# A hybrid attention and retention step: later stores of turned rows, and a later split of one left operand

## The chip, the cores and the metric

The kernel runs on one core of a Trainium2 chip. The metric is the device time of one execution in microseconds; before the change its median over three runs is 2233.36 us. The engines go by the short names of the profile: PE (matmul), PEld (weight load), DVE (VectorE), ACT (ScalarE), POOL (GpSimd), SP (SyncE, which here only issues DMAs). ACT and POOL issue DMAs too, in the order of their own instruction streams.

## What is computed

One layer of a streaming encoder, for 1024 new frames of a prompt and for 16 new frames of each of 8 running streams. One input projection gives queries, keys, values and gates for two groups of eight heads. Group A is stick-breaking attention, group B is retention with decay. Each head's output is normalised, multiplied by a gain and a gate, and all go through one output projection.

```
h = rms_norm(x, norm_pre)
q_sb, k_sb, v_sb, gate_sb, q_r, k_r, v_r, gate_r = project(h, w_in, pos)
o_sb = stick_breaking_block(q_sb, k_sb, v_sb, ...)
o_r, s = retention(q_r, k_r, v_r, s0, log_gamma)
y = concat(head_rms_norm(o_sb, g_sb) * silu(gate_sb), head_rms_norm(o_r, g_r) * silu(gate_r))
x = x + rms_norm(einsum('bte,ed->btd', y, w_out), norm_post)
```

D_MODEL is 2048, heads are 128 wide, everything is float32 in and out. The new keys, values and retention states are outputs as well.

## The kernel before

**Precision.** Each float32 operand of a large product is split into a high part (ACT, L174) and a low part (DVE, L175), and three matmuls (high by high, high by low, low by high) replace one. So each weight tile costs a load, an ACT copy, a DVE subtract, and then matmuls of 512 columns.

**Stages.** Tokens are in two groups: group 0 has prompt tiles 0 to 3 and the tile of samples, group 1 has prompt tiles 4 to 7. For each group and each head five panels run: a row panel (`project_rows`, L473: values and gates) and four column panels (`project`, L416), most often in the order retention keys, retention queries, attention queries, attention keys. Then comes the output stage: the output projection is one level of a seven-product scheme over 2 by 2 blocks (`product`, matmuls at L1306, L1309 and L1310). Products are numbered 1 to 7 and each has two halves of columns, `nh`. Their left operands are rows or sums of rows of the heads' outputs, split by `left`; their right operands are blocks or sums of blocks of the output weights, split by `load_split` two blocks ahead of use (`AHEAD` = 2).

**The planner.** All that is not a large matmul is written as generators, wrapped in `Job`. After each matmul of a panel `tick` advances a clock by one turn (by 0.75 turn in a row panel; in the output stage after every three matmuls by one, two or three turns) and lets at most one job that is due take its next step. What a step yields is the number of turns until its next step. `drain(job)` ticks until a job is done, with no matmul in between. The step only emits instructions in program order; the framework then orders each engine's stream. `pin` forbids an instruction to stand ahead of the latest large matmul at the time of its turn; it is an ordering rule and not a wait.

**The work around the first edit.** `finish` (L768) runs once per head and branch. It normalises and gates the head's rows on DVE, stores them to a scratch (`turn_out`), loads them back with 32 by 32 blocks moved (`turn_in`), transposes them on DVE (L782), multiplies by the gain (L783) and stores the turned rows to `s_y` with a DMA issued on ACT (L786). Between these are waits in turns: for group 1, 7 before `turn_out` (`D_HELD`), 16 more before `turn_in`, 13 before the transpose, 7 before the store. The tile names are `so` for attention and `ro` for retention. `drain(sb_job)` at L1230 stands in the next head's attention step, between its queries' and its keys' panel (behind both in the first head and the last two of group 1); `drain(ret_job)` at L1203 stands behind the next head's retention keys. Rows of `s_y` are read by `sum_rows` (sums of rows, L307) and by `left` (L344) in the output stage.

**The work around the second edit.** In the output stage `both` (L1463) makes the `left` jobs for a product and a list of groups. `left` loads rows into a ring (three buffers `mr` for group 0, two `yr` for group 1), yields `wait`, and then splits eight pieces, one per step, into operands named `mh`/`ml` (group 0) or `ah`/`al` (group 1); after a second piece it loads the next pair into the freed buffer. The job for product 2, group 0, starts with the first half of product 1 for group 1 (two turns after every three matmuls, eight blocks of four turns), and `all_of(ready)` drains it before product 2.

Of the kernel before, what the change touches and what calls it, by code (L numbers as in the profile page):

```python
# [47 lines left out]
D_HELD = 7  # L48
# [16 lines left out]
D_LEFT = 24  # L65
D_SUM2 = (4, 6, 26)
D_SUM3 = (3, 3, 6)
MR = 3
# [26 lines left out]
def tile_hybrid_step(  # L95
# [48 lines left out]
    wp = ctx.enter_context(tc.tile_pool(name="wp", bufs=4))  # L144
# [27 lines left out]
    def split(hi, lo, src):  # L172
        return (
            nc.scalar.activation(hi, src, AF.Copy),  # L174
            nc.vector.tensor_tensor(lo, src, hi.bitcast(F32), ALU.subtract),  # L175
        )

    def split_pre(hi, lo, src, k):
        return (
            nc.scalar.activation(hi, src, AF.Copy, scale=pre[:, k : k + 1]),  # L180
            nc.vector.scalar_tensor_tensor(  # L181
                lo, src, pre[:, k : k + 1], hi.bitcast(F32), ALU.mult, ALU.subtract
            ),
        )

    def inv_rms(pool, ssq, n, name):
        shape = list(ssq.shape)
        v = pool.tile(shape, F32, name=f"{name}v")
        r = pool.tile(shape, F32, name=f"{name}r")
        u = pool.tile(shape, F32, name=f"{name}u")  # L190
        nc.vector.tensor_scalar(v, ssq, 1.0 / n, EPS, ALU.mult, ALU.add)
        nc.scalar.activation(r, v, AF.Sqrt)
        nc.vector.reciprocal(r, r)
        nc.vector.scalar_tensor_tensor(u, r, -0.5, r, ALU.mult, ALU.mult)
        nc.vector.tensor_tensor(u, u, v, ALU.mult)
        nc.vector.scalar_tensor_tensor(r, u, 1.5, r, ALU.add, ALU.mult)
        return r

    def pin(*made):
        if anchor[0] is not None:  # L200
            for ins in made:
                tc.add_manual_dep(
                    ins.ins,
                    anchor[0].ins.name,
                    mybir.DependencyInfo(mybir.DependencyClass.NoSync, mybir.DependencyReason.SCHED_ONLY),
                    reason="not ahead of the products",
                )
# [7 lines left out]
    def tied(ins):  # L215

        if phase[0] == 0 and anchor[0] is not None:
            tc.add_manual_dep(
                ins.ins,
                anchor[0].ins.name,  # L220
                mybir.DependencyInfo(mybir.DependencyClass.NoSync, mybir.DependencyReason.SCHED_ONLY),
                reason="tied to the products",
            )
# [80 lines left out]
    def sum_rows(gi, h):  # L304
        def load(r):
            for kk in range(2):
                pin(nc.sync.dma_start(r[:, 2 * kk : 2 * kk + 2].rearrange("p a n -> p (a n)"), y_of(gi, kk * H + h)[:, :512]))  # L307

        ops = ((3, 1, 3, "a"), (1, 0, 1, "s"), (0, 3, 0, "s"), (2, 2, 0, "s"))
        return load, ops, s_s[gi][h // 2][:, h % 2]  # L310
# [3 lines left out]
    def sums(pool, items, pace, bufs):  # L314

        def fetch(load):
            r = pool.tile([P, 4, 256], F32, name="br", tag="br", bufs=bufs)
            load(r)
            return r

        r = fetch(items[0][0])
        yield pace[2]
        for i, (_, ops, dst) in enumerate(items):
            nxt = fetch(items[i + 1][0]) if i + 1 < len(items) else None
            for o, a, b, how in ops:
                pin(nc.vector.tensor_tensor(r[:, o], r[:, a], r[:, b], ALU.add if how == "a" else ALU.subtract))
                yield pace[0]
            yield pace[1]
            pin(nc.scalar.dma_start(dst, r))
            stored[0] += 1  # L330
            r = nxt
            yield pace[2]

    def left(gi, n, hi, lo, bufs, tag, deep, wait, spare=None):
        src = LEFT[n]
        raw = []

        def load(pair, r=None):
            r = bufs.tile([P, 2, 256], F32, name=tag, tag=tag, bufs=deep) if r is None else r
            if src[0] == "y":  # L340
                rows = s_y[gi][src[1] * H // 2 + pair][:, :, src[2] * 256 : src[2] * 256 + 256]
            else:
                rows = s_s[gi][pair][:, :, src[1], :]
            pin(nc.sync.dma_start(r, rows))  # L344
            raw.extend((r[:, 0], r[:, 1]))

        for pair in range(deep):
            load(pair)
        yield wait
        ahead = deep  # L350
        if spare is not None:
            load(deep, spare.pop().rearrange("p t j d -> p (t j d)")[:, :512].rearrange("p (i n) -> p i n", i=2))
            ahead += 1
            yield 0
        for h in range(HT):
            pin(*split(hi[h], lo[h], raw.pop(0)))
            if h % 2 and h // 2 + deep >= ahead and h // 2 + deep < HT // 2:
                load(h // 2 + deep)
            yield D_OP
# [37 lines left out]
    def operand(pool, tags, n, **kw):  # L397
        made = [pool.tile([P, HT, n], F32R, name=t, tag=t, **kw) for t in tags]
        return [[t[:, h] for h in range(HT)] for t in made]
# [87 lines left out]
    with ExitStack() as s1:  # L487
# [46 lines left out]
        with tc.tile_pool(name="p0", bufs=2) as p0, tc.tile_pool(name="p0s", bufs=1) as p0s, tc.tile_pool(  # L534
# [97 lines left out]
            for piece, (o, m) in enumerate(X_PIECES[:2]):  # L632
                for w in range(KT // WQ):
# [3 lines left out]
                    for j in range(WQ):  # L637
                        k = w * WQ + j
                        hi, lo = (half[w][:, j, o : o + m] for half in mov)
                        made = split_pre(hi, lo, xc[:, j, :], k)  # L640
# [54 lines left out]
        def turn_out(src, tag, q=nc.scalar, held=False):  # L695

            s = scr.tile([src.shape[1], P, P], F32, name=tag)
            store = q.dma_start(s.rearrange("k q c -> q k c"), src)
            if held:
                pin(store)  # L700
            return s
# [3 lines left out]
        def turn_in(s, raw, q, last=None):  # L705

            for i in range(4):
                tied(
                    (last if last and i == 3 else q).dma_start(  # L709
                        raw[32 * i : 32 * i + 32, :].rearrange("p (k a) -> p k a", a=32),  # L710
                        s[:, :, 32 * i : 32 * i + 32].rearrange("k (j b) a -> b (k j) a", b=32),
                    )
                )
# [44 lines left out]
        class Out:  # L758
# [9 lines left out]
            def finish(self, b, gi, h, at, oT, dst):  # L768
                rs = inv_rms(op, self.ssq, P, "o")
                for i in range(self.nt):  # L770
                    nc.vector.scalar_tensor_tensor(
                        self.o[:, i, :], self.o[:, i, :], rs[:, i : i + 1], gated[gi, h][:, at + i, b, :], ALU.mult, ALU.mult
                    )
                if gi == 1:
                    yield D_HELD
                s = turn_out(self.o, f"s_o{b}_{h}_{self.nt}_{gi}", held=gi == 1)
                yield D_TO[phase[0]] - (D_HELD if gi == 1 else 0)
                flat = self.o.rearrange("p k d -> p (k d)")
                turn_in(s, flat, back[phase[0]])
                yield D_TI[phase[0]]  # L780
                n = self.nt * P
                tied(nc.vector.transpose(oT[:, :n], flat))  # L782
                nc.vector.tensor_scalar(flat, oT[:, :n], gains[:, b, h : h + 1], None, ALU.mult)  # L783
                if gi == 1:
                    yield D_HELD
                store = nc.scalar.dma_start(dst, flat)  # L786
                if gi == 1:
                    pin(store)
# [354 lines left out]
        summed, sampled, lefts, mine = [], [], [], {}  # L1143
        held_over, spare = [], []

        def kept(i):
            return [[half[i][:, h // 2, h % 2 * 256 : h % 2 * 256 + 256] for h in range(HT)] for half in mov]
# [18 lines left out]
        for gi, g in enumerate(GROUPS):  # L1166
            tiles, n, nt = g["tiles"], g["n"], len(g["tiles"])
# [161 lines left out]
        made = collections.deque()  # L1329
# [64 lines left out]
    with ExitStack() as s3:  # L1394
        c3 = s3.enter_context(tc.tile_pool(name="c3", bufs=1))
        rp = s3.enter_context(tc.tile_pool(name="rp", bufs=1))
# [26 lines left out]
        def complete(key, c):  # L1423
            o = area(key, c)
            square(key, c, o)
            yield D_FIN
            pin(nc.vector.tensor_tensor(o, o, gpost[:, c * 512 : (c + 1) * 512], ALU.mult))
            if len(ssqs[key][1]) == 4:
                finishing[key] = Job(finish(key), D_FIN)
# [33 lines left out]
        def both(n, groups):  # L1463
            made = []
            for g in groups:
                mine[g, n] = operand(c3, ("ah", "al"), 256, bufs=2) if g else kept(at[n])
                made.append(left(g, n, *mine[g, n], *((rp, "yr", 2) if g else (wp, "mr", MR)), D_LEFT // 2))
            return made

        def jobs_of(made):  # L1470
# [28 lines left out]
        def early_rows():  # L1499
            for key in LAST[:2]:  # L1500
                load_row(key)
                yield 30

        (first,) = both(1, G1)
        more = Job(sums(fp, [sum_rows(1, h) for h in range(EARLY, H)], D_SUM3, 3), 30)
        Job(load_gpost(), 40)
# [201 lines left out]
```

## Time and profile before

| | us |
|---|---|
| median of three runs | 2233.36 |
| lowest and highest of them | 2231.7 and 2233.37 |
| the profiled execution's own time | 2233.32 |
| its span, first to last instruction | 2231.6 |
| mean clock granted to PE, share of full speed | 0.998 |

The profile describes one execution. Its span leaves out what lies around the program. "Busy" of PE is made of matmuls whose ends are modelled, and matmuls overlap, so a busy PE says that it does not wait, not that it is at its peak. Rows of the waits name who waited for whom, then the total, the number of waits and the longest. Rows of a timeline give the start, the duration, the engine (with a q where it is the engine's sequencer that issues a DMA), the line, the tiles written and read, and in brackets how long the engine was idle before and what ended that. Rows of windows give the length of the window, the busy time and the number of instructions of each engine asked for, PE's granted clock, the DMA engines' busy share and GB/s.

### The profile page before, as it was taken

What the parts mean: (1) busy time and instruction counts of PE and PEld (TensorE: products, weight loads), DVE (VectorE), ACT (ScalarE), POOL (GpSimd) and SP (SyncE); (2) the same over time, 40 slices, a digit from 0 to 9 for tenths busy, and PEclk for the clock granted to TensorE, in tenths of its full rate; (3) what the DMA queues carried; (4) which work ended last, traced back from release to release, by engine and by line L of the source; (5) the groups of instructions that cost most, each with busy time, mean ns of one, the idle gap of its engine ahead of it and who ended that gap; (6) DMA issues with size and microseconds to landing.
All of it is one profiled execution on the core that took longest, in us unless ns stands there. A gap on an engine that the chain in (4) does not pass through costs nothing. (4 is left out here: it accounts for less than half of the span.)

```text
span 2231.6 us, 34775 instructions
## 1 busy us (share of the span) xinstructions
PE 2216.6 (99%) x12046; PEld 1887.5 (85%) x12046; DVE 1263.4 (57%) x2690; ACT 920.8 (41%) x1999; POOL 424.5 (19%) x715
## 2 busy tenths in 40 slices
PE   9999999999999999999999999999999999999998
PEld 8888889798888979888788888888888888878887
DVE  5435445453544545346566666757665757656677
ACT  6424333333333333334444343443434445545563
POOL 1022131222213122221222111120202212000020
PEclk9999999999999999999999999999999999999999
DMA  8567565576656557668768787878778777865785
GB/s 295 174 199 199 178 185 181 177 193 217 178 184 184 182 176 195 217 179 289 226 197 230 229 231 221 237 229 237 229 228 223 222 233 197 241 215 166 219 224 170
DMA packets 387234, 467.83 MB, mean 210 GB/s; under 512 B 126321, under 2 KB 243825, under 8 KB 386545
## 3 DMA queue, kind: packets, MB, share of 16 engines
q1 hardware_dynamic: 258928, 291.63, 44.2%
q0 software_dynamic: 36048, 94.67, 15.6%
q10 hardware_dynamic: 92080, 79.32, 11.3%
q8 instruction: 94, 1.54, 0.3%
q14 instruction: 84, 0.68, 0.1%
HBM read 364.56 MB, written 106.95 MB: 211 GB/s over the span
## 5 line engine op out<-in xcount | busy, mean ns | idle before, releaser
L473 PE MATMUL accm<-whn,ml 128*128 128x512 f32 x1152 | 452.3, 393 | 0.0
L473 PE MATMUL accm<-whn,mh 128*128 128x512 f32 x1152 | 451.6, 393 | 0.5 <-DVE rq L519 0.5
L473 PE MATMUL accm<-wln,mh 128*128 128x512 f32 x1152 | 451.9, 392 | 0.0
L174 ACT ACTIVATE wh<-wr 128x512 fp32r<-128x512 f32 x408 | 256.7, 631 | 466.2 <-PE acc L416 191.2
L416 PE MATMUL acc<-ml,wh 128*128 128x256 f32 (+2 forms) x1536 | 446.3, 341 | 0.7 <-DVE ml L181 0.3
L416 PE MATMUL acc<-mh,wl 128*128 128x256 f32 (+2 forms) x1536 | 443.9, 340 | 0.0
L416 PE MATMUL acc<-mh,wh 128*128 128x256 f32 (+2 forms) x1536 | 441.4, 338 | 0.2
L175 DVE TENSOR_TENSOR wl<-wr,wh 128x512 fp32r<-128x512 f32 x408 | 279.4, 688 | 264.6 <-ACT wh L174 244.7
L175 DVE TENSOR_TENSOR wln<-wrn,whn 128x512 fp32r<-128x512 f32 x256 | 175.5, 688 | 285.2 <-ACT whn L174 281.5
L174 ACT ACTIVATE whn<-wrn 128x512 fp32r<-128x512 f32 x256 | 161.2, 631 | 384.4 <-PE accm L473 261.4
L416 PEld LDWEIGHTS acc<-mh,wl 128*128 128x128 f32 x1536 | 281.3, 188 | 23.8 <-issue 5.4
L416 PEld LDWEIGHTS acc<-mh,wh 128*128 128x128 f32 x1536 | 283.0, 188 | 21.0 <-ACT mh L180 0.9
L416 PEld LDWEIGHTS acc<-ml,wh 128*128 128x128 f32 x1536 | 280.3, 188 | 21.1 <-DVE ml L181 1.6
L473 PEld LDWEIGHTS accm<-whn,mh 128*128 128x128 f32 x1152 | 216.5, 188 | 44.6 <-DVE rq L519 0.9
L473 PEld LDWEIGHTS accm<-whn,ml 128*128 128x128 f32 x1152 | 216.5, 188 | 43.2 <-issue 0.8
L473 PEld LDWEIGHTS accm<-wln,mh 128*128 128x128 f32 x1152 | 216.5, 188 | 43.2 <-DVE wln L175 0.3
L745 DVE TENSOR_TENSOR_SCAN kp<-kp 128x1152 f32<-128x1152 f32 (+4 forms) x40 | 82.6, 2064 | 55.9 <-POOL kp L734 28.1
L709 POOL DMA_DIRECT2D be<-s_be x120 | 87.8, 738 | 128.2 <-DMA s_be<-be 128.2
L1306 PE MATMUL a<-wh,mh 128*128 128x512 f32 x240 | 94.7, 395 | 0.1
L1309 PE MATMUL a<-wl,mh 128*128 128x512 f32 x240 | 93.8, 391 | 0.3 <-DVE wl L175 0.2
L1310 PE MATMUL a<-wh,ml 128*128 128x512 f32 x240 | 93.6, 390 | 0.0
L734 POOL TENSOR_SCALAR_AFFINE_SELECT kp<-kp 128x128 f32<-128x128 f32 x40 | 13.8, 345 | 369.2 <-ACT kp L728 369.2
(289 smaller groups left out, 3013.2 us busy)
## 6 DMA issues: line engine op xcount, KB each, us to landing
wrn<-w_rows SPq DMA_DIRECT2D x256, 256.0 KB, 3.9
wr<-w_cols SPq DMA_DIRECT2D x255, 256.0 KB, 4.4
kcT<-cache_k POOLq DMA_DIRECT2D x64, 512.0 KB, 4.7
vc<-cache_v SPq DMA_DIRECT2D x64, 512.0 KB, 5.3
wr<-s_b SPq DMA_DIRECT2D x80, 256.0 KB, 3.4
wr<-w_out SPq DMA_DIRECT2D x80, 256.0 KB, 4.3
br<-w_out SPq DMA_DIRECT2D x64, 256.0 KB, 4.6
s_b<-br ACTq DMA_DIRECT2D x32, 512.0 KB, 4.5
```

The lines of the kernel that those rows point to most:

```text
L174: nc.scalar.activation(hi, src, AF.Copy),
L175: nc.vector.tensor_tensor(lo, src, hi.bitcast(F32), ALU.subtract),
L416: last = nc.tensor.matmul(a[:, :m], lhs[:, j, :], rhs[w][:, j, o : o + m], start=(w == 0 and j == 0 and n == 0), stop=(w == KT // WQ - 1 a ...
L473: anchor[0] = nc.tensor.matmul(banks[t], lhs[q][:, j, ts], rhs, start=(k == 0 and n == 0), stop=(k == KT - 1 and n == 2),)
L709: (last if last and i == 3 else q).dma_start(raw[32 * i : 32 * i + 32, :].rearrange("p (k a) -> p k a", a=32), s[:, :, 32 * i : 32 * i + 3 ...
L734: nc.gpsimd.affine_select(blk, blk, pattern=[[-1, P]], base=0, channel_multiplier=1, compare_op=ALU.is_gt, fill=fill,)
L745: nc.vector.tensor_tensor_scan(rev, rev, rev, 1.0, ALU.mult, ALU.bypass)
L1306: ins = nc.tensor.matmul(a, hi[k][:, ts], wh, start=first, stop=False)
L1309: nc.tensor.matmul(a, hi[k][:, ts], wl, start=False, stop=False)
L1310: anchor[0] = nc.tensor.matmul(a, lo[k][:, ts], wh, start=False, stop=last)
```

## The change

Two constants change. The store of turned rows of group 1 is emitted 14 turns after its transpose and gain instead of 7. And the `left` job of product 2 for group 0 waits 16 turns instead of 12 between its first loads and its first split; all other `left` jobs keep their wait.

```diff
@@ -782,7 +782,7 @@
                 tied(nc.vector.transpose(oT[:, :n], flat))
                 nc.vector.tensor_scalar(flat, oT[:, :n], gains[:, b, h : h + 1], None, ALU.mult)
                 if gi == 1:
-                    yield D_HELD
+                    yield 2 * D_HELD
                 store = nc.scalar.dma_start(dst, flat)
                 if gi == 1:
                     pin(store)
@@ -1464,7 +1464,8 @@
             made = []
             for g in groups:
                 mine[g, n] = operand(c3, ("ah", "al"), 256, bufs=2) if g else kept(at[n])
-                made.append(left(g, n, *mine[g, n], *((rp, "yr", 2) if g else (wp, "mr", MR)), D_LEFT // 2))
+                more = 4 if (g, n) == (0, 2) else 0
+                made.append(left(g, n, *mine[g, n], *((rp, "yr", 2) if g else (wp, "mr", MR)), D_LEFT // 2 + more))
             return made
```

## The prediction

> **What bounds the kernel now.** I read the page first, then who waited for whom on PE, then busy time by stage, then the two places that the diff touches in order of time.
>
> ```profile
> span 2231.6 us, 34775 instructions
> PE 2216.6 (99%) x12046; PEld 1887.5 (85%) x12046; DVE 1263.4 (57%) x2690; ACT 920.8 (41%) x1999; POOL 424.5 (19%) x715
> ```
> ```profile
> PE pd L945 <- DVE kp L942: 1.5, 7, 0.5
> PE pb L565 <- DVE ones L538: 1.2, 1, 1.2
> PE a L1309 <- DVE wl L175: 1.0, 3, 0.7
> PE accm L473 <- DVE rq L519: 0.5, 1, 0.5
> PE pa L999 <- DVE so L851: 0.4, 1, 0.4
> PE acc L416 <- DVE ml L181: 0.3, 1, 0.3
> ```
> ```profile
> 1980.00:2020.00 40.00, 40.00 (x177) 32.76 (x176) 18.78 (x33) 15.04 (x33) 0.00 (x0) 1.00 0.44 139
> ```
> ```profile
> 2140.00:2180.00 40.00, 40.00 (x178) 33.12 (x177) 28.81 (x75) 27.94 (x64) 13.80 (x16) 1.00 1.00 236
> ```
>
> TensorE is the limit nearly everywhere. All its waits add to 1.5 + 1.2 + 1.0 + 0.5 + 0.4 + 0.3 = 4.9 us of 2231.6 (total, times, longest in each row). The first two rows lie outside both edits: the decode of group 0 and the start-up. Of what remains, the three waits for `wl` (1.0) and the one for `rq` (0.5) lie beside an edit. A change that moves instructions of other engines and removes no matmul can win a few of these waits and no more. It can lose more, if it makes PE wait where it does not wait now. In the two windows of the output stage that are shown PE is busy for 40.00 of 40.00 us, so what is won or lost before 1980 arrives at the end whole.
>
> **Edit 1, the store.** It moves sixteen issues (eight heads, two branches) by 7 turns. A turn is one tick of the planner: one matmul of a column panel, or 4/3 of one in a row panel. No instruction and no transfer is added. So the question is what sets the place of the store today, its turn or its data.
>
> ```profile
> L786 ACTq DMA_DIRECT2D s_y<-ro x16: 326/333/358, 203.8 to 1903.0; - x16
> L786 ACTq DMA_DIRECT2D s_y<-so x16: 326/338/363, 240.7 to 1928.5; - x16
> ```
> ```profile
> L344 SPq DMA_DIRECT2D yr<-s_y x12: 517/538/610, 1941.9 to 2147.2; - x12
> ```
> ```profile
> 1248.10:1296.85 48.75, 44.92 (x192) 35.78 (x192) 1.00 0.76 222
> ```
> ```profile
> 1296.90:1309.90 13.00, 11.54 (x48) 8.71 (x48) 1.00 0.80 225
> 1309.95:1322.40 12.45, 11.38 (x49) 9.05 (x49) 1.00 0.92 253
> 1322.40:1338.30 15.90, 12.88 (x49) 8.38 (x49) 1.00 0.80 236
> ```
> ```profile
> 1343.15 0.70 DVE L782 STREAM_TRANSPOSE be<-so 128x512 f32<-128x512 f32 x1
> ```
> ```profile
> 1344.15 0.48 DVE L783 TENSOR_SCALAR so<-be,pre 128x512 f32<-128x512 f32 x1
> ```
> ```profile
> 1344.54 0.63 ACT L174 ACTIVATE whn<-wrn 128x512 fp32r<-128x512 f32 x1 [2.10 <-PE acc L416]
> 1344.70 0.33 ACTq L786 DMA_DIRECT2D s_y<-so  x1
> ```
>
> I count the attention job of one head of group 1 that is made at about 1248. The next row panel has 192 matmuls at 0.75 turn, so 144 turns, at 44.92 / 192 = 0.234 us a matmul. Three column panels of 48 follow (a row with x49 counts an edge matmul twice), so the drain at L1230 comes at turn 288, near 1338.3. By the constants the job needs 11 + 11 turns to its first scores, 3 x 39 + 42 for four tiles, 2 x 21 for the two late steps, and 7 + 16 + 13 + 7 in `finish`: 22 + 117 + 42 + 42 + 43 = 266. I add about 5 turns for rounding to 0.75 and for turns that other jobs take: the store's turn is about 271, the 31st matmul of the third column panel, some 5 us before 1338. With 14 turns it is 278, some 3 us before it. But the trace has the store at 1344.70, 0.07 us after the gains that it stores ended (1344.15 + 0.48 = 1344.63), and behind an ACT split that belongs to the next row panel, whose turn is later than either. So data sets its place, about 9 us after the new turn. The same holds in the retention branch of the next head:
>
> ```profile
> 1350.01 0.39 PE L473 MATMUL accm<-whn,mh 128*128 128x512 f32 x1
> ```
> ```profile
> 1356.97 0.48 DVE L783 TENSOR_SCALAR ro<-rkn,pre 128x512 f32<-128x512 f32 x1
> ```
> ```profile
> 1358.25 0.34 ACTq L786 DMA_DIRECT2D s_y<-ro  x1
> ```
>
> That job is made at turn 192 and needs 11 + 23 + 28 to its first scores, 9 x 5 in the retention and 43 in `finish`: 342, 6 turns into the next row panel, which starts at turn 336 and at 1350.01. Held 14 it is 13 turns in, at 4/3 x 0.234 us a turn 4.1 us: 1354.1, again before its gains end at 1357.45. If the hold did bind in some heads, the store would leave 1.6 to 2.2 us later (7 turns). What hides that is distance: the last stores leave at 1903.0 and 1928.5, and `left` loads such rows of group 1 only from 1941.9 on. I cost edit 1 at 0.
>
> Its bounds. Below nothing: there is one place where an ACT that is held up by a store reaches PE, the wait for `rq`.
>
> ```profile
> 1753.61 0.34 ACTq L786 DMA_DIRECT2D s_y<-so  x1
> 1754.05 0.63 ACT L174 ACTIVATE whn<-wrn 128x512 fp32r<-128x512 f32 x1 [2.60 <-PE acc L416]
> 1754.70 0.60 ACT L517 ACTIVATE sw<-acc 64x512 f32<-64x512 f32 x1
> ```
>
> The split and the rope copy stand behind a store there. If the store went behind them, the copy could start up to 1 us sooner and the 0.5 us of PE would go: -0.5. Above nothing: the mechanism of rival B.
>
> **Edit 2, the split of group 0 for product 2.** The job starts with the first half of product 1 for group 1, 8 blocks of 4 turns. Its first loads stay at turn 1; the first split moves from turn 13 to 17, the eighth from about 27 to 31. Eight ACT copies and eight DVE subtracts move one block later, and with them SP's fourth load, which follows the second split.
>
> ```profile
> 1966.70 0.42 ACT L174 ACTIVATE mh<-mr 128x256 fp32r<-128x256 f32 x1 [2.76 <-DMA mr<-s_y]
> 1967.03 0.61 ACT L174 ACTIVATE wh<-wr 128x512 fp32r<-128x512 f32 x1
> ```
> ```profile
> 1970.05 0.63 ACT L174 ACTIVATE wh<-wr 128x512 fp32r<-128x512 f32 x1 [2.10 <-DMA wr<-w_out]
> ```
> ```profile
> 1967.15 0.43 DVE L175 TENSOR_TENSOR ml<-mr,mh 128x256 fp32r<-128x256 f32 x1 [0.95 <-ACT mh L174]
> 1967.50 0.68 DVE L175 TENSOR_TENSOR wl<-wr,wh 128x512 fp32r<-128x512 f32 x1
> ```
> ```profile
> 1967.19 0.39 PE L1306 MATMUL a<-wh,ah 128*128 128x512 f32 x1
> 1968.24 0.50 PE L1309 MATMUL a<-wl,ah 128*128 128x512 f32 x1 [0.66 <-DVE wl L175]
> ```
> ```profile
> 1970.90 0.40 PE L1306 MATMUL a<-wh,ah 128*128 128x512 f32 x1
> 1971.46 0.50 PE L1309 MATMUL a<-wl,ah 128*128 128x512 f32 x1 [0.16 <-DVE wl L175]
> ```
>
> The first split waits for its rows: ACT sits idle 2.76 us for the load, DVE 0.95 us for ACT, and the `wl` of block 6 is queued behind that `ml`. At 0.23 us between matmuls PE was due at 1967.42 and starts at 1968.24: 0.82 us late. Block 6's weights are split at turn 16 (two blocks ahead of use). So with the first split at turn 17 they stand ahead of it, `wl` runs about 0.95 us sooner, and this stall goes: -0.82.
>
> What is late next is the first block of the second half. Its `wh` starts at 1970.05 when its load has landed; `wl` and the PE row at 1971.46 hang on that. This load was issued ahead of all that moves, and the DMA engines had little room (the last two columns are DMA share and GB/s):
>
> ```profile
> 1964.10 4.47 SPq L1323 DMA_DIRECT2D wr<-w_out  x4
> 1968.88 0.52 SPq L344 DMA_DIRECT2D mr<-s_y  x1
> ```
> ```profile
> 1960.00:1970.00 10.00, 9.35 (x40) 6.79 (x39) 8.84 (x23) 4.45 (x12) 0.00 (x0) 1.00 0.88 301
> ```
>
> PE arrives there 0.82 us sooner and waits 0.82 us longer: +0.82. After that the moved splits compete with the weights of the second half. I take 0 for that, since the weights' splits have waits for loads around them that can absorb 0.4 us. Its ends: nothing below, and above it the late fourth load may hold ACT at the seventh split in front of a weight split, for up to the length of one block, 6 x 0.23 = 1.4 us.
>
> The Trainium skill, "DMA: Bandwidth & Descriptors", section "Anatomy of one DMA — SWDGE (gpsimd) path", fits a transfer as 2.0 us plus its bytes over 436 GB/s; for 256 KB that is an estimate of 2.6 us. By that the load of 1964.10 would land at 1966.7, the second stall would not hang on it, and the sum would be -0.8. This trace does not agree: its consumer began at 1970.05, after a wait for it.
>
> **Sum.** 0 for edit 1, -0.8 + 0.8 for edit 2: 0 on the span of 2231.6, and so on the 2233.3 of the profiled execution (1.7 us lie around the span), which is the median of the three runs (2233.4; 2231.7 to 2233.4). Small wins are likelier than small losses by the chances below, so I shade it by 0.2 and say **2233.2**.
>
> **Rivals.**
>
> A, a few waits are won. The second stall does not take the gain back, because the queue of transfers ahead of that load clears sooner. For: both PE waits are for `wl`, and DMA share is 0.88, not 1. Against: nothing ahead of the load changes its place. With the 0.5 of `rq`: -0.8 to -1.3, about 2232.1. The skill's formula would give this too.
>
> B, slower. The hold pushes `finish` past the drain at L1230. From there each missing turn is run with no matmul under it, and the retention job, which is in its middle then, loses cover between its PE, DVE, PE steps. It decides once more than 288 - 278 = 10 turns are lost beyond the 5 that I counted. Price: up to 7 turns x 0.234 = 1.6 us in each of 7 heads, 11 us: 2244. Against: twice the lost turns that I count would still fit.
>
> C, slower by little. The late fourth load holds ACT in front of a weight split: +1.4, about 2234.7.
>
> D, edit 1 does nothing, because data and not the turn places the store. That is inside my forecast.
>
> **How the numbers follow.** Forecast (2232.5 to 2234) 0.66, A 0.17, C 0.12, B 0.05. The range reaches over A and C and adds part of the spread of the runs, 1.7 us: **2230.7 to 2235.2**. A measurement of this kernel can tell about 0.2%, 4.5 us, from no change. The waits within reach (1.0 + 0.5 + 0.4) are less than that, so faster by more gets 0.02, the far end of A; slower by more is B, 0.05; the same 0.93.
>
> **What would show it.** Sixteen stores of group 1 at L786, each still at or after the end of its L783; retention matmuls around a drain spaced as now (else B). The PE wait near 1968 gone and the one near 1971.5 grown by as much (else A, or C if a new one follows it). PE without a gap from 1985 on. I would be wrong if PE waits where no row has a wait now, or if the order on ACT and DVE changes far from the two edits.

## The result, and the profile after

The changed kernel takes **2237.22 us** (median of 19 executions, 2234.96 to 2238.93) beside 2233.1 us (19, 2231.53 to 2235.43) for the kernel before. The ratio is 1.0017, with a 95% interval of 1.0011 to 1.0023: slower by 4.1 us. That is less than the 0.2% that the prediction calls no change, but it lies 2.0 us above the top of the forecast range.

The profiled execution of the changed kernel took 2235.51 us, 2.2 more than the profiled one before (2233.32), and lies near the low end of its 19. So this trace can show about half of the loss at most. Its head, and then its waits of PE (total, times, longest):

```profile
span 2233.8 us, 34771 instructions
PE 2216.3 (99%) x12046; PEld 1887.6 (85%) x12046; DVE 1263.8 (57%) x2690; ACT 920.7 (41%) x1999; POOL 424.0 (19%) x715
```
```profile
PE pa L848 <- DVE kp L811: 2.0, 1, 2.0
...
PE a L1309 <- DVE wl L175: 1.0, 3, 0.6
PE acc L416 <- ACT mh L180: 0.7, 2, 0.4
PE a L1306 <- ACT wh L174: 0.5, 1, 0.5
...
PE rs L980 <- DVE rq L521: 0.2, 1, 0.2
```

Busy times are as before. The large new wait is one of 2.0 us in **one** place of the attention of group 1, at L848. The rows left out are as before. Of the smaller new rows two are no sign of the edits. The 0.7 us at L180 stand in the first 100 us, ahead of both edits, and every other run but the kernel before shows 0.4 to 1.5 us there. The 0.5 us at L1306 stand at 1931.81, some 31 us before the first loads of edit 2's job, and e1, e3 and e4 below, which leave edit 2 out, have 0.2 to 0.6 us there:

```profile
1931.81 0.50 PE L1306 MATMUL a<-wh,mh 128*128 128x512 f32 x1 [0.51 <-ACT wh L174]
```

The windows (length, PE busy and its matmuls, clock, DMA share, GB/s) put the wait of L848 between 1400 and 1430 us and clear the stretches around it:

```profile
1000.00:1400.00 400.00, 400.00 (x2082) 1.00 0.79 233
1400.00:1430.00 30.00, 30.00 (x156) 1.00 0.99 260
1430.00:1955.00 525.00, 523.65 (x2524) 1.00 0.79 225
```
```profile
1000.00:1400.00 400.00, 400.00 (x2081) 1.00 0.79 234
1400.00:1430.00 30.00, 27.96 (x145) 1.00 0.89 238
1430.00:1955.00 525.00, 523.64 (x2523) 1.00 0.78 225
1980.00:2020.00 40.00, 39.76 (x174) 1.00 0.43 141
```

The first fence is the kernel before, the second the changed one. In 30 us PE lost 2.04 us; before and behind that, in group 1, nothing. The last row (40.00 of 40.00 before) has a small wait of the output stage, 0.23 us at 1983.18.

**The place near 1425 us.** These are the timeline rows of the kernel before, and then of the changed one: the transpose of L811, and on PE the last projection matmul and the matmuls of L848 that need the transpose.

```profile
1425.12 1.25 DVE L811 STREAM_TRANSPOSE kp<-be 128x1024 f32<-128x1024 f32 x1 [2.31 <-DMA be<-s_be]
```
```profile
1426.24 0.39 PE L416 MATMUL acc<-mh,wh 128*128 128x512 f32 x1
1426.47 1.12 PE L848 MATMUL pa<-vo,kp 128*128 128x128 f32 x8
```
```profile
1426.30 1.25 DVE L811 STREAM_TRANSPOSE kp<-be 128x1024 f32<-128x1024 f32 x1 [3.65 <-DMA be<-s_be]
```
```profile
1425.17 0.39 PE L416 MATMUL acc<-mh,wl 128*128 128x512 f32 x1
1427.60 1.16 PE L848 MATMUL pa<-vo,kp 128*128 128x128 f32 x8 [2.04 <-DVE kp L811]
```

Before, the transpose ended at 1425.12 + 1.25 = 1426.37 and PE reached L848 at 1426.47: a margin of 0.10 us, of which the rows of waits show nothing. After, PE is there at 1425.17 + 0.23 = 1425.40, and the transpose ends at 1427.55. On PE the eight matmuls of L848 stand behind 102 projection matmuls of this head instead of 106, so four earlier (4 x 0.23 = 0.9 us). The transfer that the transpose waits for lands later, which makes the remaining 1.3 us of this pair of traces.

Two traces exaggerate the second part. Nine of the fourteen traces have the old order, with 106: there the transpose ends between 0.10 us before PE arrives and 0.55 us behind, and PE's wait is at most 0.45 us. Five have the order with 102 (the change, e1, e4, e5, e9): there it ends 1.35 to 2.15 us behind. Counted from the last matmul of the row panel, it ends after 28.2 us on average in the nine and 28.7 us in the five. So 0.9 us of the wait come from the order in every case, and on average 0.5 us from the later landing.

**The place near 1970 us.** SP's issues in the output stage, first of the kernel before (the prediction shows the two rows ahead of these: four weight loads from 1964.10, the fourth `mr` at 1968.88), then of the changed one; then what SP waited for at L344 between 1960 and 1986 us, changed kernel:

```profile
1969.50 4.38 SPq L1323 DMA_DIRECT2D wr<-w_out  x4
1973.93 1.18 SPq L344 DMA_DIRECT2D yr<-s_y  x2
```
```profile
1965.06 4.49 SPq L1323 DMA_DIRECT2D wr<-w_out  x5
1972.22 0.52 SPq L344 DMA_DIRECT2D mr<-s_y  x1
1972.85 1.32 SPq L1323 DMA_DIRECT2D wr<-w_out  x2
1974.21 1.18 SPq L344 DMA_DIRECT2D yr<-s_y  x2
1975.49 7.99 SPq L1323 DMA_DIRECT2D wr<-w_out  x6
```
```profile
SPq L344 <- DVE ml L175: 2.6, 1, 2.6
```
```profile
SPq L344 <- DVE ml L175: 0.2, 1, 0.2
```

The last fence is the kernel before (1960 to 1985 us). The fourth load refills the buffer of the first pair, so it waits for the second split, `ml`. It waited 0.2 us; now it waits 2.6 us, and SP issues nothing between 1969.55 and 1972.22. Five weight loads now go ahead of it instead of four, so the fifth comes no later than before. What comes later is the fourth load itself, and behind it the eighth weight load, which feeds the last block of the second half: it now follows the two `yr` loads, at 1975.49, and stood ahead of them before. In this trace the ACT split of that block starts as its load lands, and PE waits for its low part at 1983.18 (0.23 us):

```profile
1981.77 0.63 ACT L174 ACTIVATE wh<-wr 128x512 fp32r<-128x512 f32 x1 [1.02 <-DMA wr<-w_out]
```

That wait alone proves nothing: e1, e3 and e5, without edit 2, have one of 0.22 to 0.23 us between 1980 and 1983 too. What edit 2 costs is read from the experiments. The Trainium skill, "Perfetto Trace Analysis", section "Summary: the profiler window per engine type", lists the actual data movement of a DMA that SP issues as hidden from the profile. The trace agrees: the row of the fourth load is 0.52 us long, from 1972.22, and the split that waits for its rows starts at 1975.67. The 2.6 us of waiting are not in the row either.

### The profile page after: what moved, and what is told of

It is laid out like the page before. It is cut to its first block, busy times and chain, and to the rows that moved or that the text cites. A ratio compares the mean times of both kernels' runs of the same rounds, so it can differ in the third digit from the quotient of the medians.

```text
span 2233.8 us, 34771 instructions
## 1 busy us (share of the span) xinstructions
PE 2216.3 (99%) x12046; PEld 1887.6 (85%) x12046; DVE 1263.8 (57%) x2690; ACT 920.7 (41%) x1999; POOL 424.0 (19%) x715
## 4 chain that ended last, share of the span: by engine, by line
PE 93%; DMA 3%; DVE 2%; issue 1%; ACT 1%; DVEq 0%; POOL 0%; ACTq 0%; SPq 0%; POOLq 0%
PE accm L473 35%; PE acc L416 33%; PE a L1309 4%; PE a L1310 4%; PE a L1306 4%; PE pa L848 2%; PE z L821 2%; PE pd L953 1%; PE zc L892 1%; DMA wr<-w_out 1%; PE rs L980 1%; PE pa L999 1%; PE pS L1016 1%; PE pa L1006 1%; DMA mr<-s_s 1%
## 5 line engine op out<-in xcount | busy, mean ns | idle before, releaser
L1306 PE MATMUL a<-wh,mh 128*128 128x512 f32 x240 | 94.8, 395 | 0.5 <-ACT wh L174 0.5
```

Source lines behind the costliest of these rows:

```text
L1306: ins = nc.tensor.matmul(a, hi[k][:, ts], wh, start=first, stop=False)
```

## The experiments

Three theories. **T**: the planner lets one job per turn take a step, so moving the store's step gives its old turn to another job and takes a turn from one; the order of the other work changes, and that makes the wait of L848. **S**: the later stores cost something themselves. **C**: edit 2 loses time since the fourth load is late and holds the weight loads in SP's queue. The expectations of e1 and e2 also name **L**: all of the loss is edit 2's. The experiments ran in three groups of four, each group beside its own runs of the kernel before (medians 2233.6, 2234.2 and 2234.27; 32 or 33 executions); each experiment has 11. What is "over before" is a difference of these medians.

A list of the planner's turns, written while the program is built, shows where T begins: turn, the turn at which the step was due, the job, and the wait that it yields. It is the second head of group 1. The numbers behind the names are lines of the program with the list built in, ten higher than in kernel.py. First the kernel before, then one in which that head's attention store alone is held:

```
4086.0 at 4086.0 due 2 residuals:405 wait 76 P1
4087.0 at 4086.0 due 2 sb_branch:1147>finish:795 wait None P1
4088.0 at 4087.0 due 1 sums:338 wait 26 P1
```
```
4086.0 at 4086.0 due 1 residuals:405 wait 76 P1
4087.0 at 4087.0 due 1 sums:338 wait 26 P1
...
4093.0 at 4093.0 due 1 sb_branch:1147>finish:795 wait None P1
```

The store was due together with another job's step, went one turn later, and pushed the weight sums (`sums`, L314) from 4087 to 4088. Held, it frees that turn. From there on the sums run ahead of where they were: by one turn, then two, in the end up to seven (eight in the changed kernel), and in the third head the attention job's steps come one turn earlier too: the one that emits these matmuls of L848 takes turn 4365 instead of 4366. Why one turn in the list becomes four matmuls in the order on PE was not followed up.

**e1, edit 1 alone.**

```diff
                 if gi == 1:
-                    yield D_HELD
+                    yield 2 * D_HELD
```

> Edit 1 alone (hold of 14 turns, the left operand as before). Theory T (turns): the planner lets one job step per turn, so moving the store's step by 7 turns moves the steps that it collided with, by one turn and then more, and with them the order of the PE stream in group 1; the attention matmuls of a head's last tile (L848) then stand ahead of their transposed weights (L811) and PE waits. All of the loss is in this edit: 2 to 5 us slower than before, with waits of L848 for L811. Theory L (left): the loss comes from edit 2; then this one is within 1 us of before.

2236.95 us (2234.36 to 2238.05), 1.001 (1.0001 to 1.0019): +3.3. Its waits of PE have the same new row, with 1.4 us:

```profile
PE pa L848 <- DVE kp L811: 1.4, 1, 1.4
```

L falls: edit 1 alone loses. The interval allows 0.2 to 4.2 us.

**e2, edit 2 alone.**

```diff
-                made.append(left(..., D_LEFT // 2))
+                made.append(left(..., D_LEFT // 2 + 4 * ((g, n) == (0, 2))))
```

> Edit 2 alone. Theory T: within 1 us of before; the PE wait near 1968 gone and the next one longer by about as much. Theory L: 2 to 5 us slower.

2235.44 us (2234.17 to 2239.74), 1.001 (1.0002 to 1.0019): +1.8. Both expectations missed: T had no loss of edit 2, L nearly all of it. Both edits lose, and 3.3 + 1.8 us can make up the whole 4.1, given that each is uncertain by about 2 us. The rows of DVE, ACT and PE, and the wait of SP:

```profile
1970.66 0.43 DVE L175 TENSOR_TENSOR ml<-mr,mh 128x256 fp32r<-128x256 f32 x1 [1.97 <-ACT mh L174]
```
```profile
1969.69 0.63 ACT L174 ACTIVATE wh<-wr 128x512 fp32r<-128x512 f32 x1 [1.79 <-DMA wr<-w_out]
1970.23 0.40 ACT L174 ACTIVATE mh<-mr 128x256 fp32r<-128x256 f32 x1
...
1975.96 0.42 ACT L174 ACTIVATE mh<-mr 128x256 fp32r<-128x256 f32 x1 [2.06 <-DMA mr<-s_y]
...
1976.76 0.41 ACT L174 ACTIVATE mh<-mr 128x256 fp32r<-128x256 f32 x1
1977.07 1.66 ACT L174 ACTIVATE wh<-wr 128x512 fp32r<-128x512 f32 x3
```
```profile
1977.74 0.50 PE L1306 MATMUL a<-wh,ah 128*128 128x512 f32 x1 [0.50 <-ACT wh L174]
1978.46 0.50 PE L1309 MATMUL a<-wl,ah 128*128 128x512 f32 x1 [0.23 <-DVE wl L175]
```
```profile
SPq L344 <- DVE ml L175: 2.9, 1, 2.9
```

The chain can be read off. The second split of `mh` (1970.23) now stands behind a weight split that waits 1.79 us for its own load. Its `ml` ends at 1971.09, and SP issues the fourth load at 1971.12 (1968.88 before). The seventh split needs these rows: ACT sits idle for 2.06 us until they land (1975.96). Behind the seventh and the eighth split stands the weight split of the fifth block of the second half (1977.07), and PE waits for it at 1977.74 and 1978.46, where the kernel before has no wait. The weights themselves were not late: their load is the fifth, issued by 1968.07, ahead of the hold, and such loads of this trace landed within 6.1 us. PE's wait stands more than 6 us behind its cause, in another line and behind another engine.

**e3, the store 14 turns after its gain, the other jobs' turns as before.** For group 1 the store goes on a list behind the gain, and the list is emptied at the 14th turn without using one up. The step still takes its turn after 7, and does nothing in it; in the list of turns no step moves.

```diff
-        clock[0] += by
+        clock[0] += by; [aside.pop(0)[1]() for _ in list(aside) if aside[0][0] <= clock[0]]
...
-                    yield D_HELD
+                    aside.append((clock[0] + 2 * D_HELD, lambda: pin(nc.scalar.dma_start(dst, flat)))); ... yield D_HELD; return
```

> The store is issued 14 turns after its gain, but aside from the planner's jobs: finish still takes its turn after 7 turns, as before, so no other step moves. Theory T: within 1 us of before. Theory S (store): the later place of the store on ACT and in the DMA queues costs the time; then 2 to 5 us slower, as in the whole change.

2234.14 us (2233.35 to 2235.6), 1.0 (0.9992 to 1.0009): +0.5. S falls: the later stores cost nothing that shows, though in this trace three of the sixteen leave 1.9 to 4.3 us behind their gain (before, none more than 0.80 us).

**e4, the store after 7 turns from the list, the step's last turn after 14.**

```diff
...
-                    yield D_HELD
+                    aside.append((clock[0] + D_HELD, lambda: pin(nc.scalar.dma_start(dst, flat)))); ... yield 2 * D_HELD; return
```

> The reverse: the store is issued after 7 turns, aside from the jobs, and finish takes its last turn after 14, so the other steps move as in the change. Theory T: 2 to 5 us slower than before, like edit 1 alone. Theory S: within 1 us of before.

2235.69 us (2234.36 to 2238.09), 1.001 (1.0001 to 1.0019): +2.1, with the wait of L848 again:

```profile
1427.26 1.16 PE L848 MATMUL pa<-vo,kp 128*128 128x128 f32 x8 [1.25 <-DVE kp L811]
```

The store stays and the turn moves, and the loss is there. T holds, S does not.

**e5, one store of the sixteen held, and e6, the fifteen others.**

```diff
-                    yield D_HELD
+                    yield 2 * D_HELD if (b, h) == (0, 1) else D_HELD
```

> Edit 1 for one store of the sixteen, the one of the second attention head (h = 1) of the first batch; the other fifteen stay at 7 turns. Theory T (the step's turn moves the planner's other jobs, and from this head on the group's sums come up to 8 turns earlier, which brings four matmuls of the fourth attention job, L848, in front of a transpose that waits for a transfer): this one store carries the loss of edit 1, 2 to 3.4 us over before, and TensorE waits 1 to 2 us at L848 for the transpose of L811. Rival (the loss is spread over the sixteen stores, each of them a later transfer): a sixteenth of it, about 0.2 us.

> The counterpart: the other fifteen second-group stores wait 14 turns, the one of the second attention head stays at 7. Theory T: the order of the work before the eighth head is that of before, so the time is within 1 us of before and the wait at L848 is missing. Rival (spread over the stores): fifteen sixteenths of the loss, 2 to 3 us over before.

e5 took 2236.93 us (2234.9 to 2238.4), 1.0011 (1.0002 to 1.002): +2.7 from a single store. e6, with the two waits exchanged, took 2234.41 us (2231.51 to 2236.99), 1.0002 (0.9993 to 1.001): +0.2. The timeline rows of L848 in e5 and in e6:

```profile
1427.80 0.94 PE L848 MATMUL pa<-vo,kp 128*128 128x128 f32 x6 [1.72 <-DVE kp L811]
```
```profile
1426.52 1.16 PE L848 MATMUL pa<-vo,kp 128*128 128x128 f32 x8
```

Both theories had a number for each, and T's came. (The attention job concerned is the group's third, not the fourth, as the expectation has it.) Edit 1 loses where one collision of two due steps is undone. In e6 the list has moved steps too, of other jobs by up to three turns from the third head on, and none of that shows as a loss: a moved turn costs where it reaches an operand with a small margin. The wait of L848, 1.2 to 2.0 us in the five traces, is less than the medians' 2.1 to 3.3 us, but within their intervals.

**e7, edit 2 with the first two splits, and so the fourth load, at their old turns.**

```diff
-            yield D_OP
+            yield D_OP + 4 * ((gi, n, h) == (0, 2, 1))
```

> Edit 2 without its effect on the fourth load: the first two of the eight splits of the left operand, and with them the fourth load of its ring, stay at their old turns; the six other splits come four turns later. Theory C (the fourth load waits for the second split and holds the weight loads behind it in SP's queue, so TensorE waits for weights near 1977 us): within 1 us of before, the stall near 1968 us stays or shrinks, no wait near 1977. Rival (the later splits themselves stand in front of the weights' splits on ScalarE and VectorE): 1 to 2 us over before, with the new waits near 1972 to 1983 still there.

2234.07 us (2232.75 to 2236.91), 1.0001 (0.9992 to 1.001): -0.1. SP's wait is 0.2 us again and the stall of 1968 is back:

```profile
1968.57 0.50 PE L1309 MATMUL a<-wl,ah 128*128 128x512 f32 x1 [0.51 <-DVE wl L175]
1978.77 0.50 PE L1309 MATMUL a<-wl,ah 128*128 128x512 f32 x1 [0.23 <-DVE wl L175]
```

The small wait near 1978.8 is as long as those that e1, e3 and e5 have there without edit 2, so it is no price of the six later splits.

**e8, edit 2 whole, the fourth load in a free buffer of the other ring.** It is issued just ahead of the first split and waits for none.

```diff
+                free = [rp.tile([P, 2, 2, P], F32, name="yr", tag="yr", bufs=2)] if (g, n) == (0, 2) else None
-                made.append(left(..., D_LEFT // 2))
+                made.append(left(..., D_LEFT // 2 + 4 * (free is not None), free))
```

> Edit 2 as it is (all eight splits four turns later), but the fourth load goes into a free buffer of another ring and is issued just ahead of the first split, so that it waits for no split and holds nothing in SP's queue. Theory C: within 1 us of before, at best 0.9 us faster (the stall near 1968 gone, no new wait near 1977). Rival (the later splits themselves): 1 to 2 us over before, as in the run with edit 2 alone.

2233.54 us (2232.2 to 2234.89), 0.9998 (0.9989 to 1.0007): -0.7. All eight splits are late, only the fourth load is not, and the loss is gone. A hold of SP as such does not cost it: in e8 SP waits 1.8 us for `al` and 1.2 us for `wl` at L344, for other loads. The wait near 1978 is gone too, but the one at the first block of the second half stays:

```profile
1971.20 0.51 PE L1306 MATMUL a<-wh,ah 128*128 128x512 f32 x1 [1.18 <-ACT wh L174]
1971.93 0.50 PE L1309 MATMUL a<-wl,ah 128*128 128x512 f32 x1 [0.22 <-DVE wl L175]
```

**e9 to e12: the change, edit 2 alone and its spare-buffer form once more, and both edits without their side effects** (e12 joins the edits of e3 and e8), side by side.

> The changed kernel once more, beside the next three on one chip. Theories T and C together: about 4 us over before (2 to 3 from the moved turns, 1 to 2 from the late fourth load), and a second profile that shows the wait of TensorE at L848 for the transpose of L811 (1.4 to 2.2 us) and the one at L1306 near 1977 us again. Rival (the waits are an accident of one profiled execution): other waits in other places.

> Edit 2 alone once more, beside the kernel with the spare buffer. Theory C: 1 to 2 us over before again, wait near 1977 us. Rival (edit 2 costs nothing and the first run of it was a chance): within 0.7 us of before and of the next kernel.

> Edit 2 with the fourth load in a free buffer once more, so that the two can be set against each other on one chip. Theory C: within 1 us of before, and 1 to 2 us below the run with edit 2 alone beside it. Rival: equal to it.

> Both edits as the change words them, without their two side effects: each second-group store is issued 14 turns after its gain from a list of its own, so that the planner's other jobs keep their turns, and the fourth load goes into a free buffer. Theories T and C: within 1 us of before, 3 to 4 us below the change. Rival (the later stores or the later splits cost something by themselves): 2 us or more over before.

| | us (range) | ratio (95%) | over before |
|---|---|---|---|
| e9, the change | 2237.59 (2236.12 to 2242.19) | 1.0016 (1.0007 to 1.0025) | +3.3 |
| e10, edit 2 alone | 2235.65 (2233.55 to 2237.01) | 1.0004 (0.9995 to 1.0014) | +1.4 |
| e11, with the spare buffer | 2232.9 (2231.97 to 2235.35) | 0.9996 (0.9987 to 1.0005) | -1.4 |
| e12, both mended | 2233.75 (2232.24 to 2234.68) | 0.9995 (0.9986 to 1.0004) | -0.5 |

In e9 SP waited 2.9 us at L344. Below are PE's wait of L848, and PE in the last block of the second half, which waits for its weights as in the first trace of the change:

```profile
PE pa L848 <- DVE kp L811: 1.4, 1, 1.4
```
```profile
1983.67 0.50 PE L1306 MATMUL a<-wh,ah 128*128 128x512 f32 x1 [0.33 <-ACT wh L174]
```

So the waits are no accident of one execution, though the expectation had the last one near 1977. In e10 SP waited 2.8 us, and the chain of e2 came again, near 1980:

```profile
1978.19 0.42 ACT L174 ACTIVATE mh<-mr 128x256 fp32r<-128x256 f32 x1 [2.11 <-DMA mr<-s_y]
```
```profile
1979.97 0.50 PE L1306 MATMUL a<-wh,ah 128*128 128x512 f32 x1 [0.52 <-ACT wh L174]
```

By itself e10 is not clear of no change, but e11 beside it is 2.75 us lower (1 to 2 were expected), with the splits of both at the same turns: eight of e11's eleven executions are below the lowest of e10's. e12 makes both edits and loses nothing. No version is shown to be faster than the kernel before: the best interval still holds 1.

For edit 2 a sum over all traces helps, since one trace of this stretch says little. I add up how much later than the usual pitch of 0.227 us PE's matmuls start between 1950 and 1990 us (those over 0.1 us late). The six traces without edit 2 (before, e1, e3 to e6) give 0.5 to 2.1 us, mean 1.4; the four with it (the change, e2, e9, e10) 1.6 to 3.7, mean 2.7; e7 gives 2.1; the three with the spare buffer 1.7 to 2.0, mean 1.8. From 1975 us on, behind the first block of the second half, they part more clearly: 0.2 to 0.8 without edit 2, 0.8 to 1.3 with it, 0.6 in e7 and nothing in the three with the spare buffer.

## Why the prediction failed

**Edit 1, "I cost edit 1 at 0": the store was right, the step was not.** "So data sets its place" held for the store shown. It is the one whose step e5 moves; in the changed kernel's trace it still follows its gain at once (1344.35 + 0.48 = 1344.83):

```profile
1344.35 0.48 DVE L783 TENSOR_SCALAR so<-be,pre 128x512 f32<-128x512 f32 x1
```
```profile
1344.86 0.35 ACTq L786 DMA_DIRECT2D s_y<-so  x1
```

Nine more of the sixteen stores leave within 0.1 us of their gain there. The other six leave 0.5 to 4.0 us behind it. In the kernel before four left 0.2 to 0.8 us behind, the prediction's second example among them, at 0.80. So data does not place every store; but e3 shows that such delays cost nothing that can be measured.

The step that failed is the count of turns: "I add about 5 turns for rounding to 0.75 and for turns that other jobs take". It counts the turns that others take from this job and not the turns that this job takes from others. A step that issues one small DMA still fills a turn of a queue in which one job is served per turn. Its price, 0 in the sum, was +2.1 (e4), +2.7 (e5) and +3.3 (e1). The sentence on what would make the prediction wrong, "if PE waits where no row has a wait now", describes what came; but nothing in the sum looked for places with a small margin. The wait table does not show them: the margin of 0.10 us near 1425 has no row.

**Edit 2, -0.8: right.** The stall near 1968 is gone in the changed kernel, e2 and e8. **+0.8: right in kind.** The first block of the second half waits longer; in the changed kernel by 0.57 at `wl`, 0.73 us behind the pitch, against 0.33 before:

```profile
1972.85 0.50 PE L1309 MATMUL a<-wl,ah 128*128 128x512 f32 x1 [0.57 <-DVE wl L175]
```

The fit of the Trainium skill that the prediction quotes ("DMA: Bandwidth & Descriptors", section "Anatomy of one DMA — SWDGE (gpsimd) path") is for DMAs that gpsimd issues; this load is issued by SP. By the fit it would have landed early and the gain would have stayed; this trace and e8 (1.18 us of wait for `wh` there) speak against it.

**"I take 0 for that": the step that failed.** The term was +1.8 (e2) and +1.4 (e10). Rival C had it, with the cause (the late fourth load), the path (ACT held at the seventh split in front of a weight split) and with 1.4 us about the price: so it came in e2 and e10. In the two traces of the change the seventh split waits only 0.7 and 0.6 us, and PE waits for a weight load that SP issued late, a path that the prediction does not have. The error was to price C at a chance of 0.12 and the sum at 0, on the ground that the waits for loads around the weights' splits "can absorb 0.4 us". The delay was larger: the second split did not move by four turns of six matmuls, 6 x 0.23 = 1.4 us, but from 1968.43 to 1970.66 in e2, 2.2 us, since it came to stand behind a weight split that waits for its load. The prediction named the fourth load as moved, and did not follow it on SP.

**Rival A** came in part: the 0.5 us of `rq` is gone from the changed kernel's waits, as "-0.5" in the bounds had it, and gone or down to 0.2 us in all six traces in which edit 1 moves turns. In e4 the store keeps its turn and the wait is gone too, so the moved turns win it and not the store. The 2.0 us at L848 outweigh it. **Rival B** is refuted: from 1000 to 1400 us PE is busy for 400.00 of 400.00 us, and the list of turns shows no turn that the hold left without a matmul. **Rival D** is half right: ten of the sixteen stores leave as soon as their data are there, and the edit still does something.

**The range** took its upper end from rival C and the spread of the runs. It gave edit 1 an upper end only through rival B, and none for a wait at a place that has none today. The loss of edit 2 alone, 1.4 to 1.8 us, would have stayed within it, beside the 2233.1 us of the kernel before; edit 1 took the time past its end.

What stays open: why the transfer of L811 lands later, by 0.5 us on average, once the sums have moved. Other transfers are issued at other times around it; which of them is in its way was not tried.

## What to carry to other kernels

Where a planner serves one job per turn, a moved step changes every job that was due with it or behind it; compare the two orders far from the edit before costing the edit at nothing, and look for operands that arrive just in time, since the wait table shows only those that are late already. When a load moves, follow it on both sides: on the queue that issues it, where a load that waits for a buffer holds what is issued behind it, and on the engine that takes it up, where a split that waits for late rows holds the splits behind it. The engine that pays stands several microseconds later in another line.

## What the runs showed of the hardware

A wait of PE costs more than its row. After a stall the first matmul is shown with 0.50 us instead of 0.39, and the next one starts 0.33 us behind it instead of 0.23 (changed kernel):

```profile
1983.18 0.50 PE L1309 MATMUL a<-wl,ah 128*128 128x512 f32 x1 [0.23 <-DVE wl L175]
1983.51 0.39 PE L1310 MATMUL a<-wh,al 128*128 128x512 f32 x1
```

So each such stall adds about 0.11 us that no wait has. And the stretch from 1950 to 1990 us varies by itself: in the six traces without edit 2 PE was late there by 0.5 to 2.1 us, a spread as large as what edit 2 costs.
